# A feed-forward's second pair of column chunks in seven products, with block sums moved from VectorE to GpSimd

## Chip, core and metric

The kernel runs on one core of a Trainium2 chip. The time is device microseconds (us) from the first to the last instruction of one execution, with a small fixed part around it. Three runs of the kernel before took 1752.14, 1753.64 and 1753.94 us; the median is 1753.64 us.

## What is computed

Two layers, each with two feed-forwards around a mixer, all in float32, for 512 tokens of 1024 channels; a feed-forward is 2816 wide. This document is about the feed-forwards, four in the program:

```python
def swiglu_ffn(x, w_gu, w_down):
    a, u = jnp.split(x @ w_gu, 2, axis=-1)
    return (jax.nn.silu(a) * u) @ w_down
...
x = layer_norm(DEEPNORM_ALPHA * x + 0.5 * swiglu_ffn(x, ffn1_w_gu[l], ffn1_w_down[l]), ln1_g[l], ln1_b[l])
x = layer_norm(DEEPNORM_ALPHA * x + hybrid_mixer(x, w_in[l], w_out[l], ...), ln2_g[l], ln2_b[l])
x = layer_norm(DEEPNORM_ALPHA * x + 0.5 * swiglu_ffn(x, ffn2_w_gu[l], ffn2_w_down[l]), ln3_g[l], ln3_b[l])
```

## The kernel before

**Three matmuls for one.** Each operand is held as a high part (`uh` for weights, `xh` for x) and the rest of it (`ul`, `xl`). `split` (L171) makes them: ScalarE casts the high part (L173), VectorE subtracts it from the source (L174). A product is then three matmuls per 128x128 block of weights (`mm3`, L188 to L190): high by high, high by low, low by high.

**A feed-forward's first half.** It goes over 11 pairs of column chunks (`fp`). A pair is two chunks of 128 columns of the gate weights `a`, and two of the up weights `u`; the two arrive as two tiles `raw` of 1 MB, for which there are two buffers, and are split into `units` (six pairs of buffers). Loads are issued by SyncE as a buffer of `raw` comes free. An ordinary product of one chunk with all of x takes 8 x 3 matmuls, 512 tokens wide, or twice as many that are 256 wide.

**Seven products.** For the pairs in `SEVEN`, `glu7` takes a 2x2 block scheme (channels in halves, tokens in halves, columns in halves) with seven block products in place of eight, each of 4 x 3 matmuls 256 wide, once for `a` and once for `u`: 168 matmuls. It needs sums of the weights' blocks (tile `S`, four of 128x512 for each `raw`, L321 to L326), and sums of the blocks of x (`Th`, `Tl`; T1 to T4). The latter are made once in a feed-forward by `sums_of_x`: four tensors `xh + xl` (L556), four subtractions (L560), four splits. They lie in a part of `hT` that is written late.

**The start of a feed-forward**, where the change is. x arrives in four blocks of 128 tokens from the norm of the stage before, 0 to 3. For each, VectorE adds the residual (L513), takes statistics (L515, L518, L519), GpSimd makes the inverse root `rs` (L521), VectorE finishes `Y` (L522, L525), TensorE transposes it (L488), and `xh`, `xl` are split from the PSUM bank. So that TensorE need not wait for blocks 2 and 3, pair 0 (and half of pair 1) is taken on the first 256 tokens first: 96 narrow matmuls. Then come the transposes of blocks 2 and 3, or of 3 alone, then 192 narrow matmuls (the rest of pair 0, both halves of two chunks of pair 1), then the last two chunks of pair 1 in 48 matmuls that are 512 wide. From pair 2 on it is seven products. At its first matmul stand four throw-away ones (L460), which mark where pair 1 ends.

**Order of the work.** Every engine takes its instructions in a fixed order, which the tile framework made when the program was built, with a wait on other engines where one is needed: an instruction that waits holds up all behind it on its engine. GpSimd's list held, around a feed-forward, only the `rs` of the norms, and later the DMAs that add blocks of the down weights (L394). The 8 banks of PSUM are handed on: a transposed block needs a bank that an earlier gate (`silu(a) * u`, L630 and L631) has read. The first gate also waits until the norm before has let go of the memory that its parameters `ln` lie in, since the pools of the two stages share it.

Of the kernel before, what the change touches and what calls it, by code (L numbers as in the profile page):

```python
# [99 lines left out]
class Trunk:  # L100
# [199 lines left out]
    def seven_items(self, a, u):  # L300
# [16 lines left out]
        def s12(q):  # L317
            def go(v, hi, lo):
                s = sums[q] = self.spool.tile([P, 4, KC // 2, P], F32, tag="S", name=self.nm("S"), bufs=2)
                a11, a12, a21, a22 = blocks(v)  # L320
                self.nc.vector.tensor_add(s[:, 0], a21, a22)  # L321
# [214 lines left out]
    def ffn(self, g_, b, out=None):  # L536
        nc, tc, W = self.nc, self.tc, self.W
        with ExitStack() as ctx:
# [8 lines left out]

            def sums_of_x():

                x = hT[:, NF - KC :, :]  # L550
                B = [[x[:, i * H : (i + 1) * H, j * 256 : (j + 1) * 256] for j in range(2)] for i in range(2)]
                for i in range(2):
                    ks = slice(i * H, (i + 1) * H)
                    for j in range(2):
                        ts = slice(j * 256, (j + 1) * 256)
                        nc.vector.tensor_add(B[i][j], self.xh[:, ks, ts].bitcast(F32), self.xl[:, ks, ts].bitcast(F32))  # L556
                        yield 1
                for i, (dst, p_, q_) in enumerate(((B[0][0], B[0][1], B[0][0]), (B[0][1], B[1][1], B[0][1]),
                                                   (B[1][1], B[1][1], B[0][0]), (B[1][0], B[1][0], B[1][1]))):
                    nc.vector.tensor_sub(dst, p_, q_)  # L560
                    self.split(Th[:, i], Tl[:, i], dst)
                    yield 1
# [640 lines left out]
```

## Time and profile before

| | |
|---|---|
| median of the runs | 1753.64 us |
| the profiled execution | 1752.16 us, its span 1750.4 us |
| TensorE busy, granted clock | 1739.2 us, 0.999 |
| VectorE, ScalarE, GpSimd busy | 1415.5, 927.6, 182.7 us |

The profile is one execution as the hardware recorded it. A row of a timeline is: start and length in us, engine (PE is TensorE, DVE VectorE, ACT ScalarE, POOL GpSimd, SPq the queue of SyncE), line, operation, what it writes and reads, how many were merged, and in brackets for how long the engine had stood idle and who ended that. Operations of one engine that follow each other overlap a little in these records, so that two merged rows show better than one what each costs. A row of the windows gives each engine's busy time, with the number of instructions, in a stretch of the span. A row of the groups ends in busy us and mean ns of one.

The four feed-forwards are called F1 to F4 here. F1 follows the input, F2 and F4 a mixer, F3 the down projection of F2.

### The profile page before, as it was taken

To read this page: it belongs to the slowest core of one execution; us is meant where nothing else is said; L and a number is where in the kernel's file an instruction comes from. 1 tells how busy PE (TensorE), PEld (TensorE's weight loads), DVE (VectorE), ACT (ScalarE), POOL (GpSimd) and SP (SyncE) were. 2 spreads that over 40 slices of the span, in tenths; PEclk is the share of its full clock that TensorE was granted. 3 is DMA by queue.
4 is the path that set the end of the run, shared out by engine and by line. 5 is a ranking of instruction groups with operands and counts; after the bars stand their busy time and mean duration, and the time that the engine had idled before them with its cause. 6 is when DMAs were issued, how large, how long until landed. Compare 5 with 4: busy or idle time off the path is not lost.

```text
span 1750.4 us, 29200 instructions
## 1 busy us (share of the span) xinstructions
PE 1739.2 (99%) x11946; PEld 1580.1 (90%) x11946; DVE 1415.5 (81%) x1975; ACT 927.6 (53%) x1456; POOL 182.7 (10%) x154
## 2 busy tenths in 40 slices
PE   9999999999999999999999999999999999999998
PEld 9999988887789999998899999889877899999886
DVE  7888888856757889879898988988567587988887
ACT  5455656378712455555435556554785234555551
POOL 0000032111111000014000000312011110000231
PEclk9999999999999999999999999999999999999999
DMA  6234389323222243279423334982233123334891
GB/s 193 97 108 134 126 214 220 98 86 95 73 74 73 74 141 101 97 219 217 130 67 109 115 97 157 219 190 91 92 89 97 49 91 103 98 98 144 209 212 48
DMA packets 163765, 216.34 MB, mean 124 GB/s; under 512 B 5168, under 2 KB 116528, under 8 KB 163632
## 3 DMA queue, kind: packets, MB, share of 16 engines
q1 hardware_dynamic: 141872, 172.55, 30.5%
q0 software_dynamic: 21760, 41.95, 13.2%
q8 instruction: 93, 1.52, 0.4%
q14 instruction: 40, 0.33, 0.1%
HBM read 212.38 MB, written 2.10 MB: 123 GB/s over the span
## 4 chain that ended last, share of the span: by engine, by line
PE 48%; DVE 2%; DMA 0%; issue 0%; ACT 0%; POOLq 0%; DVEq 0%; ACTq 0%
PE ps L188 15%; PE ps L189 15%; PE ps L190 15%; PE ps L488 0%; DMA raw<-in_ffn_w_gu_dram 0%; PE ps L1030 0%; PE ps L995 0%; PE ps L1082 0%; PE ps L1022 0%; DVE Y L522 0%; PE ps L1044 0%; DVE ul L174 0%; DVE st L515 0%; DVE Y L513 0%; DVE xl L174 0%; DVE Y L525 0%
## 5 line engine op out<-in xcount | busy, mean ns | idle before, releaser
L188 PE MATMUL ps<-xh,uh 128*128 128x256 f32 (+1 forms) x1616 | 476.0, 295 | 0.0
L189 PE MATMUL ps<-xl,uh 128*128 128x256 f32 (+1 forms) x1616 | 473.0, 293 | 0.5 <-DVE xl L174 0.4
L190 PE MATMUL ps<-xh,ul 128*128 128x256 f32 (+1 forms) x1616 | 473.1, 293 | 0.4 <-DVE ul L174 0.4
L173 ACT CAST uh<-raw 128x1024 fp32r<-128x1024 f32 (+1 forms) x274 | 236.6, 884 | 233.3 <-PE ps L189 127.7
L174 DVE TENSOR_TENSOR ul<-raw,uh 128x1024 fp32r<-128x1024 f32 (+1 forms) x274 | 273.6, 1014 | 56.8 <-ACT uh L173 56.4
L188 PE MATMUL ps<-Th,uh 128*128 128x256 f32 x1152 | 318.0, 276 | 0.0
L189 PE MATMUL ps<-Tl,uh 128*128 128x256 f32 x1152 | 318.0, 276 | 0.0
L190 PE MATMUL ps<-Th,ul 128*128 128x256 f32 x1152 | 318.0, 276 | 0.0
L188 PEld LDWEIGHTS ps<-xh,uh 128*128 128x128 f32 x1616 | 304.1, 188 | 10.5 <-issue 1.6
L190 PEld LDWEIGHTS ps<-xh,ul 128*128 128x128 f32 x1616 | 303.5, 188 | 10.3 <-DVE ul L174 0.8
L189 PEld LDWEIGHTS ps<-xl,uh 128*128 128x128 f32 x1616 | 304.3, 188 | 9.1 <-DVE xl L174 0.9
L188 PE MATMUL ps<-uh,xh 128*128 128x512 f32 x720 | 285.2, 396 | 0.5 <-ACT xh L173 0.5
L189 PE MATMUL ps<-ul,xh 128*128 128x512 f32 x720 | 282.6, 392 | 0.0
L190 PE MATMUL ps<-uh,xl 128*128 128x512 f32 x720 | 281.0, 390 | 0.0
L173 ACT CAST uh<-S 128x1024 fp32r<-128x1024 f32 x144 | 151.3, 1051 | 144.0 <-PE ps L189 140.3
L189 PEld LDWEIGHTS ps<-Tl,uh 128*128 128x128 f32 x1152 | 216.3, 188 | 0.0
L188 PEld LDWEIGHTS ps<-Th,uh 128*128 128x128 f32 x1152 | 216.2, 188 | 0.0
L190 PEld LDWEIGHTS ps<-Th,ul 128*128 128x128 f32 x1152 | 216.2, 188 | 0.0
L174 DVE TENSOR_TENSOR ul<-S,uh 128x1024 fp32r<-128x1024 f32 x144 | 176.0, 1222 | 48.9 <-ACT uh L173 48.4
L394 POOL DMA_DIRECT2D R<-in_ffn_w_down_dram x80 | 97.1, 1217 | 999.8 <-DVE ul L174 912.3
L174 DVE TENSOR_TENSOR ul<-R,uh 128x1024 fp32r<-128x1024 f32 x120 | 145.5, 1223 | 31.5 <-ACT uh L173 31.2
L173 ACT CAST uh<-R 128x1024 fp32r<-128x1024 f32 x120 | 124.8, 1047 | 75.1 <-DMA R<-in_ffn_w_down_dram 36.4
(147 smaller groups left out, 2379.9 us busy)
## 6 DMA issues: line engine op xcount, KB each, us to landing
raw<-in_ffn_w_gu_dram SPq DMA_DIRECT2D x86, 1024.0 KB, 5.3
R<-in_ffn_w_down_dram POOLq DMA_DIRECT2D x80, 512.0 KB, 7.9
raw<-in_w_in_dram SPq DMA_DIRECT2D x18, 1024.0 KB, 5.2
R<-in_ffn_w_down_dram SPq DMA_DIRECT2D x16, 1024.0 KB, 6.2
raw<-in_ffn_w_down_dram SPq DMA_DIRECT2D x12, 1024.0 KB, 7.2
R<-in_ffn_w_down_dram SPq DMA_DIRECT2D x8, 512.0 KB, 4.2
raw<-in_w_in_dram SPq DMA_DIRECT2D x8, 512.0 KB, 5.9
raw<-in_w_out_dram SPq DMA_DIRECT2D x8, 512.0 KB, 6.1
```

Of the source, the lines that this page charges most:

```text
L173: a = self.nc.scalar.copy(hi, src)
L174: b = self.low = self.nc.vector.tensor_sub(lo, src, hi.bitcast(F32))
L188: keep(mm(out, ah, bh, start=start, stop=False, **kw))
L189: keep(mm(out, ah, bl, start=False, stop=False, **kw))
L190: keep(mm(out, al, bh, start=False, stop=stop, **kw))
L394: self.nc.gpsimd.dma_start(src, rows(i, j, g * 2, 2), accum_op=ALU.add))
```

## The change

- Pair 1 joins `SEVEN`. Its two products on the first half of the tokens, for `a` and for `u` (48 narrow matmuls), are taken before the transposes of blocks 2 and 3 (in F2 and F4: after all transposes, before the second half of pair 0). The other ten follow the second half of pair 0.
- Pair 1's eight weight sums (L321 to L326) go to GpSimd, in all four feed-forwards. Those of pairs 2 to 10 stay on VectorE.
- Three of the four `xh + xl` go to GpSimd (`whole`, L551): two once blocks 0 and 1 are there, the third with blocks 2 and 3. One stays on VectorE.
- `sums_of_x` makes T1 and T2 first, with a spare tile, then T3, then T4, and `glu7` takes C's product with T1 ahead of A's with T2. T1 hangs on GpSimd's third sum.
- The gate's scratch tile is 256 wide and has the buffers of `s21`, not `Q`.

```diff
-SEVEN = (2, 3, 4, 5, 6, 7, 8, 9, 10)
+SEVEN = (1, 2, 3, 4, 5, 6, 7, 8, 9, 10)
...
-    def seven_items(self, a, u):
+    def seven_items(self, a, u, eng):
...
-                self.nc.vector.tensor_add(s[:, 0], a21, a22)
-                self.nc.vector.tensor_sub(s[:, 1], s[:, 0], a11)
+                eng.tensor_add(s[:, 0], a21, a22)
+                eng.tensor_sub(s[:, 1], s[:, 0], a11)
...
-                self.nc.vector.tensor_sub(s[:, 2], a11, a21)
-                self.nc.vector.tensor_sub(s[:, 3], a12, s[:, 1])
+                eng.tensor_sub(s[:, 2], a11, a21)
+                eng.tensor_sub(s[:, 3], a12, s[:, 1])
...
-            if fp == 0:
-                items += [a[0], u[0], a[1], u[1]]
-            else:
-                items += self.seven_items(a, u) if fp in SEVEN else a + u
+            items += self.seven_items(a, u, self.nc.gpsimd if fp == 1 else self.nc.vector) if fp in SEVEN else [a[0], u[0], a[1], u[1]]
...
+            def whole(eng, i, j):
+                ks, ts = slice(i * H, (i + 1) * H), slice(j * 256, (j + 1) * 256)
+                eng.tensor_add(B[i][j], self.xh[:, ks, ts].bitcast(F32), self.xl[:, ks, ts].bitcast(F32))
+
             def sums_of_x():
...
+                whole(nc.gpsimd, 0, 1)
+                whole(nc.vector, 1, 1)
+                nc.vector.tensor_sub(B[0][0], B[0][1], B[0][0])
+                self.split(Th[:, 0], Tl[:, 0], B[0][0])
+                nc.vector.tensor_sub(spare, B[1][1], B[0][0])
+                self.split(Th[:, 2], Tl[:, 2], spare)
+                yield 1
+                nc.vector.tensor_sub(B[0][1], B[1][1], B[0][1])
+                self.split(Th[:, 1], Tl[:, 1], B[0][1])
+                yield 2
+                nc.vector.tensor_sub(B[1][0], B[1][0], spare)
+                self.split(Th[:, 3], Tl[:, 3], B[1][0])
+                yield 1
...
+                yield
                 us = W.get()
                 u22 = W.get()
                 for m in range(2):
                     C.append(self.ps())
                     u = W.get() if m else us
+                    product(C[m], u, 0, T1)
+                    nc.scalar.copy(Q[m][:, 2], C[m][:, :256])
                     product(A[m], u, 1, T2, False)
                     nc.scalar.copy(Q[m][:, 1], A[m][:, :256])
-                    product(C[m], u, 0, T1)
-                    nc.scalar.copy(Q[m][:, 2], C[m][:, :256])
...
+            us = [W.get() for _ in range(4)]
+            self.pin = False
+            au = [us[0:2], us[2:4]]
+            self.finish(self.pend[:2])
+            for i in range(2):
+                whole(nc.gpsimd, i, 0)
+            for c in range(2):
+                glu(au[c], c, 0, 256)
+            ahead = glu7(1)
+            next(ahead)
+            self.finish(self.pend[2:])
+            self.pend = []
+            xs = self.spawn(sums_of_x(), 0)
+            self.run(xs)
+            for c in range(2):
+                glu(au[c], c, 256, SEQ)
+                W.done(2)
+            self.finish([xs])
+            for _ in ahead:
+                pass
+            for fp in range(2, NFP):
```

How this moves instructions is seen at three places. GpSimd at the start of F3, before: the four `rs` of the norm behind F2 (blocks 0, 1, 2, 3) stand together, between the DMAs of F2 and F3.

```order
L394 DMA R_8337<-in_ffn_w_down_dram 128x2x512
L521 TENSOR_TENSOR rs_8845<-mv_8842,mhalf 128x1
L521 TENSOR_TENSOR rs_8868<-mv_8865,mhalf 128x1
L521 TENSOR_TENSOR rs_9011<-mv_9008,mhalf 128x1
L521 TENSOR_TENSOR rs_9034<-mv_9031,mhalf 128x1
L394 DMA R_11585<-in_ffn_w_down_dram 128x2x512 x2
```

The same place now, from the `rs` of block 1 on (`raw_9028` and `raw_9060` are pair 1's `a` and `u`, `hT_9166` holds the sums of x).

```order
L518 TENSOR_TENSOR rs_8986<-mv_8983,mhalf 128x1
L321 TENSOR_TENSOR S_9307<-raw_9028 128x512
L325 TENSOR_TENSOR S_9307<-raw_9028 128x512
L322 TENSOR_TENSOR S_9307<-S_9307,raw_9028 128x512
L326 TENSOR_TENSOR S_9307<-raw_9028,S_9307 128x512
L551 TENSOR_TENSOR hT_9166<-xh,xl 128x4x256 x2
L321 TENSOR_TENSOR S_9446<-raw_9060 128x512
L325 TENSOR_TENSOR S_9446<-raw_9060 128x512
L322 TENSOR_TENSOR S_9446<-S_9446,raw_9060 128x512
L326 TENSOR_TENSOR S_9446<-raw_9060,S_9446 128x512
L518 TENSOR_TENSOR rs_9127<-mv_9124,mhalf 128x1
L518 TENSOR_TENSOR rs_9150<-mv_9147,mhalf 128x1
```

All eight weight sums and two sums of x stand between the `rs` of block 1 and that of block 2.

VectorE in F2, before, from the last gate of pair 0's first half on: the sums of x and of the next weights, each made on VectorE itself.

```order
L631 SCALAR_TENSOR_TENSOR hT_5623<-ps_5694,Q_5757 128x256
L321 TENSOR_TENSOR S_5946<-raw_5610 128x512
L174 TENSOR_TENSOR xl<-ps_5743,xh 128x4x128
L174 TENSOR_TENSOR xl<-ps_5750,xh 128x4x128
L556 TENSOR_TENSOR hT_5623<-xh,xl 128x4x256 x2
L560 TENSOR_TENSOR hT_5623<-hT_5623 128x4x256
L322 TENSOR_TENSOR S_5946<-S_5946,raw_5610 128x512
L560 TENSOR_TENSOR hT_5623<-hT_5623 128x4x256
L174 TENSOR_TENSOR Tl_5625<-hT_5623,Th_5624 128x1024
```

The same place now, up to the split of T2 and T3; L557 waits for GpSimd's third sum of x.

```order
L551 TENSOR_TENSOR hT_5680<-xh,xl 128x4x256
L557 TENSOR_TENSOR hT_5680<-hT_5680 128x4x256
L600 TENSOR_TENSOR Q_5821<-Q_5821,ps_5820 128x256
L174 TENSOR_TENSOR ul_5848<-S_5849,uh_5847 128x1024
L174 TENSOR_TENSOR Tl_5682<-hT_5680,Th_5681 128x1024
L174 TENSOR_TENSOR ul_5888<-raw_5653,uh_5887 128x512
L174 TENSOR_TENSOR ul_5888<-raw_5659,uh_5887 128x512
L600 TENSOR_TENSOR Q_5861<-Q_5861,ps_5860 128x256
L559 TENSOR_TENSOR hT_5680<-hT_5680 128x4x256
L562 TENSOR_TENSOR hT_5680<-hT_5680 128x4x256
L174 TENSOR_TENSOR ul_5959<-S_5960,uh_5958 128x1024
L174 TENSOR_TENSOR Tl_5682<-hT_5680,Th_5681 128x1024 x2
```

Nine instructions now stand behind the wait for GpSimd and ahead of T2's split.

ScalarE in F1, before, from the first unit of pair 1 on: the four casts of blocks 2 and 3 come right behind two casts of weights.

```order
L173 CAST uh_176<-raw_168 128x1024
L173 CAST uh_180<-raw_168 128x1024
L173 CAST xh<-ps_292 128x4x128
L173 CAST xh<-ps_299 128x4x128
L173 CAST xh<-ps_306 128x4x128
L173 CAST xh<-ps_313 128x4x128
```

Now (`raw_168` and `raw_174` are pair 1's `a` and `u`, `S_322` the sums of `a` that GpSimd makes):

```order
L173 CAST uh_176<-raw_168 128x1024
L173 CAST uh_180<-raw_174 128x1024
L596 COPY Q_294<-ps_292 128x256
L173 CAST uh_320<-S_322 128x1024
L596 COPY Q_334<-ps_332 128x256
L173 CAST uh_360<-raw_168 128x512
L173 CAST uh_360<-raw_174 128x512
L173 CAST xh<-ps_367 128x4x128
L173 CAST xh<-ps_374 128x4x128
L173 CAST xh<-ps_381 128x4x128
L173 CAST xh<-ps_388 128x4x128
```

Two copies and three casts of weights, one of GpSimd's sums, are now ahead of the casts of x; F3 has the same order.

More of the change, by code (lines that the diff above doesn't have):

```diff
@@ L546, in ffn @@
             Tl = gp.tile([P, 4, H, 256], F32R, name=self.nm("Tl"))
-            def sums_of_x():
[L550 to L562, printed above, removed]
+            x = hT[:, NF - KC :, :]
+            B = [[x[:, i * H : (i + 1) * H, j * 256 : (j + 1) * 256] for j in range(2)] for i in range(2)]
+            spare = hT[:, NF - KC - H : NF - KC, :256]
+            def whole(eng, i, j):
+                ks, ts = slice(i * H, (i + 1) * H), slice(j * 256, (j + 1) * 256)
+                eng.tensor_add(B[i][j], self.xh[:, ks, ts].bitcast(F32), self.xl[:, ks, ts].bitcast(F32))
+            def sums_of_x():
+                whole(nc.gpsimd, 0, 1)
[11 more added lines that the diff above has]
+                yield 1
             def product(out, u, ui, b, new=True):
@@ L587, in glu7 @@
                     u = W.get()
-                    if fp == SEVEN[0] and m == 0:
+                    if fp == SEVEN[1] and m == 0:
                         self.lead(A[m], u)
@@ L628, in gate @@
             def gate(f, a, u, t0, t1):
[L629 to L632 removed]
+                sa = gp.tile([P, 256], F32, tag="s21", name=self.nm("s21"), bufs=2)
+                nc.scalar.activation(sa, a[:, :256], AF.Silu)
@@ L634, in glu @@
+                nc.vector.scalar_tensor_tensor(out=hT[:, f, t0:t1], in0=u[:, :256], scalar=0.5,
+                                               in1=sa, op0=ALU.mult, op1=ALU.mult)
             def glu(au, f, t0, t1):
                 a, u = self.ps(), self.ps()
-                self.projs(a[:, : t1 - t0], au[0], t0, t1)
-                self.projs(u[:, : t1 - t0], au[1], t0, t1)
+                self.projs(a[:, :256], au[0], t0, t1)
+                self.projs(u[:, :256], au[1], t0, t1)
                 gate(f, a, u, t0, t1)
-            for fp in range(NFP):
-                if fp == 0:
-                    us = [W.get() for _ in range(6)]
-                    self.pin = False
-                    au = [us[0:2], us[2:4]]
-                    self.finish(self.pend[:2])
-                    more = []
-                    for t0 in (0, 256):
-                        for c in range(2):
-                            glu(au[c], c, t0, t0 + 256)
-                            if t0:
-                                W.done(2)
-                        self.finish(self.pend[2:])
-                        if not t0:
-                            xs = self.spawn(sums_of_x(), 1)
-                        self.pend = []
-                        more.append(self.ps())
-                        self.projs(more[-1][:, :256], us[4], t0, t0 + 256)
-                    W.done()
-                    continue
-                if fp == 1:
-                    a1, u0 = us[5], W.get()
-                    for i in range(2):
-                        t0 = i * 256
-                        u = self.ps()
-                        self.projs(u[:, :256], u0, t0, t0 + 256)
-                        gate(2, more[i], u, t0, t0 + 256)
-                    W.done()
-                    u1 = W.get()
-                    glu((a1, u1), 3, 0, SEQ)
-                    W.done(2)
-                    continue
@@ L675, in ffn @@
                     self.split(*(v.rearrange("p g f t -> p (g f) t") for v in hv), hT[:, HALF : HALF + 4, :256])
-                if fp in SEVEN:
-                    self.finish([xs])
-                    glu7(fp)
-                    continue
-                a0, a1, u0 = W.get(), W.get(), W.get()
-                glu((a0, u0), fp * 2, 0, SEQ)
-                W.done(2)
-                u1 = W.get()
-                glu((a1, u1), fp * 2 + 1, 0, SEQ)
-                W.done(2)
+                for _ in glu7(fp):
+                    pass
             gctx.close()
```

4 lines of the change are left out of this document (removed).

## Prediction

> **What bounds the kernel now.** I read the page first: TensorE's share, and whether its dearest matmuls wait; then the windows of single stages, for what a matmul costs in each.
>
> ```profile
> span 1750.4 us, 29200 instructions
> PE 1739.2 (99%) x11946; PEld 1580.1 (90%) x11946; DVE 1415.5 (81%) x1975; ACT 927.6 (53%) x1456; POOL 182.7 (10%) x154
> L188 PE MATMUL ps<-Th,uh 128*128 128x256 f32 x1152 | 318.0, 276 | 0.0
> ...
> 100.00:150.00 50.00, 50.00 (x444) 50.00 (x443) 44.53 (x68) 28.37 (x43) 0.00 (x0) 1.00 0.29 93
> 584.51:595.71 11.20, 11.20 (x50) 9.03 (x49) 4.91 (x8) 2.69 (x4) 0.00 (x0) 1.00 0.57 187
> ```
>
> TensorE is busy 1739.2 of 1750.4 us, and its matmuls on `Th` have no idle time (0.0) ahead of them. So the kernel is bound by the number of matmuls, and whatever idles TensorE for a moment goes straight to the end: behind a feed-forward's start nothing has slack to give it back. In the steady stage of seven products (100 to 150) VectorE is busy 44.5 of 50 us, so it has little to spare either.
>
> A narrow matmul (256 tokens) costs 50 / 443 = 0.113 us. The window from 584.51 to 595.71 is F2's 48 wide ones (512 tokens): 11.20 / 48 = 0.233 us, somewhat more than two narrow ones.
>
> **What the change saves.** Pair 1 takes 96 narrow matmuls and 48 wide ones now: 96 x 0.113 + 11.20 = 22.05 us. In seven products it takes 168 narrow ones: 168 x 0.113 = 18.98 us. That is 3.07 us in each feed-forward, 12.3 us in four, if no wait is added.
>
> **What it puts on GpSimd.** Eight weight sums and three sums of x, per feed-forward. GpSimd makes none today; the nearest rows are its products in the mixer, of 512 and of 256 elements.
>
> ```profile
> L974 POOL TENSOR_TENSOR sw<-sw,retS 128x512 f32<-128x512 f32 x16 | 20.8, 1298 | 152.7 <-ACT sw L972 152.7
> L974 POOL TENSOR_TENSOR sw<-sw,ropeS 128x256 f32<-128x256 f32 x16 | 11.9, 745 | 46.4 <-ACT sw L972 46.4
> L321 DVE TENSOR_TENSOR S<-raw 128x512 f32<-128x512 f32 x72 | 49.6, 689 | 1.6 <-DMA raw<-in_ffn_w_gu_dram 0.3
> ...
> 842.32 2.35 DVE L174 TENSOR_TENSOR ul<-R,uh 128x1024 fp32r<-128x1024 f32 x2
> 8.40 1.28 DVE L174 TENSOR_TENSOR xl<-ps,xh 128x512 fp32r<-128x512 f32 x2
> ```
>
> A weight sum (512) costs GpSimd 1.30 us; a sum of x (1024) by the same slope 1.30 + 2 x (1.298 - 0.745) = 2.40 us, an estimate from these two rows. Eight and three are 17.6 us. On VectorE, back to back, a 512 costs 1.28 - 0.69 = 0.60 us and a 1024 costs 2.35 - 1.22 = 1.13 us, so VectorE is relieved of 8 x 0.60 + 3 x 1.13 = 8.2 us. That would be worth having where it is late, were the two engines free of each other. These rows say they are not:
>
> ```profile
> 374.96 0.69 DVE L973 TENSOR_TENSOR rr<-ps,ropeC 128x512 f32<-128x512 f32 x1 [1.68 <-ACT sw L972]
> 375.65 1.21 DVE L174 TENSOR_TENSOR ul<-raw,uh 128x512 fp32r<-128x512 f32 x1
> ...
> 375.00 1.31 POOL L974 TENSOR_TENSOR sw<-sw,ropeS 128x512 f32<-128x512 f32 x1 [4.77 <-ACT sw L972]
> ...
> 548.23 1.28 DVE L522 SCALAR_TENSOR_TENSOR Y<-Y,mv,ln 128x1024 f32<-128x1024 f32 x1
> 548.39 1.52 POOL L521 TENSOR_TENSOR rs<-mv,mhalf 128x1 f32<-128x1 f32 x1 [12.28 <-DVE mv L519]
> 557.12 1.27 DVE L522 SCALAR_TENSOR_TENSOR Y<-Y,mv,ln 128x1024 f32<-128x1024 f32 x1
> 557.35 1.46 POOL L521 TENSOR_TENSOR rs<-mv,mhalf 128x1 f32<-128x1 f32 x1 [7.43 <-DVE mv L519]
> ```
>
> The split at 375.65 reads two tensors from SBUF and takes 1.21 us where a 512 takes 0.69: it ends at 376.86, which is 0.55 us after GpSimd's product ended (376.31). It got nothing done beside GpSimd. L973, which reads PSUM and one tensor from SBUF, took its usual 0.69 under the same product. The other way round, `rs` ends 0.40 us after VectorE's L522 (549.51 to 549.91) and 0.42 after it (558.39 to 558.81), whichever head start L522 had. So an operation of VectorE with two inputs in SBUF and one of GpSimd run one after the other. I take that for all of the 11 new ones: weights' splits, sums, L522 and L525 are of that kind, splits and gates out of PSUM are not.
>
> [...]
>
> **F3, walked on the trace's clock.** The rows that it starts from and is compared with:
>
> ```profile
> 871.05 2.00 ACT L173 CAST uh<-raw 128x1024 fp32r<-128x1024 f32 x2 [5.18 <-DMA raw<-in_ffn_w_gu_dram]
> 879.54 1.45 POOL L521 TENSOR_TENSOR rs<-mv,mhalf 128x1 f32<-128x1 f32 x1 [16.16 <-DVE mv L519]
> 887.09 1.28 DVE L525 SCALAR_TENSOR_TENSOR Y<-Y,rs,ln 128x1024 f32<-128x1024 f32 x1
> 887.71 1.91 PE L488 MATMUL ps<-ident,Y 128*128 128x128 f32 x16
> 888.45 0.66 ACT L630 ACTIVATE Q<-ps 128x256 f32<-128x256 f32 x2 [14.44 <-PE ps L488]
> 872.95 1.06 ACT L173 CAST xh<-ps 128x512 fp32r<-128x512 f32 x2
> 922.93 0.64 PE L460 MATMUL ps<-uh 128*128 128x256 f32 x4
> ```
>
> GpSimd can start when pair 1's `a` lands, 871.0. Ahead of block 2's `rs` stand 8 x 1.30 + 2 x 2.40 = 15.2 us, and VectorE's two splits and L522 (L519 in the new file) get between: 2 x 1.13 + 1.2 = 3.5. So 889.7, and `rs` is out at 890.1 where it was out at 881.0. VectorE waits for it, and block 3's statistics' end is queued behind: 1.2 for block 2's finish, 0.2 for the mean, 1.2 for L522, 0.4 for `rs`, 1.2 for the finish: 894.3, where L525 ended at 888.4. The gates wait for this (`ln`'s memory), the transposes for the gates' banks. On ScalarE then, in its order: two gates 0.7, copy 0.3, a cast 0.95, copy 0.3, two casts of 512 0.5 each, two of x at 0.5: VectorE's third `xl`, which the second half's second matmul needs, ends near 900.1. TensorE, with 48 matmuls more ahead of it, is through at 887.7 + 48 x 0.113 = 893.1: it is late by 7.0 us, of which transposes fill 1.7 (887.71 to 889.4). Behind it stand 96 + 120 matmuls: 216 x 0.113 = 24.4, so 924.5 against 922.93 (L460). F3: **+1.6 us**. Without any blocking, 3.5 fall away and the path is 921.0: -1.9.
>
> **F2 and F4**, by F2's rows:
>
> ```profile
> 544.05 1.27 DVE L174 TENSOR_TENSOR xl<-ps,xh 128x512 fp32r<-128x512 f32 x2
> 558.91 1.28 DVE L525 SCALAR_TENSOR_TENSOR Y<-Y,rs,ln 128x1024 f32<-128x1024 f32 x1
> 561.02 1.03 PE L488 MATMUL ps<-ident,Y 128*128 128x128 f32 x8
> 595.71 0.64 PE L460 MATMUL ps<-uh 128*128 128x256 f32 x4
> ```
>
> Two sums of x go from 544.65 to 550.6 (2 x 2.40, a split of 1.13 between); L522, `rs` and block 2's finish follow, to 553.6. Block 3: 0.6 + 0.6 + 1.13 + 0.6 + 1.13 + 0.2, then 1.2 + 0.4, then a weight sum of 1.30 that gets in first, then 1.2: 562.0 (558.91 + 1.28 = 560.2 today). The transposes lose 1.0. GpSimd, from 559.5, has 8 x 1.30 + 2.40 = 12.8 with 3.5 of VectorE between: its last sum, for T1, is done at 575.8. L557 to 576.9; the nine behind it are 2 x 0.34 + 3 x 1.13 + 2 x 0.60 + 2 x 1.13 = 7.5; T2's split 1.13: 585.5. TensorE, from 562.0, has 0.8 of transposes and 48 + 96 + 12 matmuls (17.6) ahead of T2: 580.4. It waits 5.1, then 108 matmuls, 12.2: 597.7 against 595.71. F2: **+2.0**, and F4, in the same order, the same. Without blocking T2 is ready at 579.6, and F2 ends at 591.8: -3.9.
>
> **F1.**
>
> ```profile
> 12.58 1.23 DVE L174 TENSOR_TENSOR ul<-raw,uh 128x1024 fp32r<-128x1024 f32 x1 [0.95 <-ACT uh L173]
> 19.74 2.00 ACT L173 CAST uh<-raw 128x1024 fp32r<-128x1024 f32 x2 [1.89 <-DMA raw<-in_ffn_w_gu_dram]
> 20.10 1.91 PE L488 MATMUL ps<-ident,Y 128*128 128x128 f32 x16
> 55.61 0.64 PE L460 MATMUL ps<-uh 128*128 128x256 f32 x4
> ```
>
> Two sums of x (4.8) hold up the splits of pair 0, whose second (12.58 + 1.23 = 13.8) frees the buffer for pair 1: it ends between 13.9 and 16.2, and pair 1, here at 19.7, comes 0.1 to 2.3 later. Today the transposes cover that load at 20.10; now pair 1's products stand ahead of them and wait, to 22.3 (19.85, a weight sum of 1.30 and the split's 1.13). The first `a` ends at 25.0, `u`'s split, behind three weight sums, at 26.05; 48 matmuls are through at 28.5, the transposes at 30.2. On VectorE each of two splits of weights waits behind a sum (1.30 + 0.6, twice), then three `xl`: 34.1. 216 matmuls more: 58.5 against 55.61, **+2.9** (+4.0 if the load is at its late end; -0.4 without blocking).
>
> **Sum.** 2.9 + 2.0 + 1.6 + 2.0 = +8.5 on the profiled execution's 1752.16: 1760.7. That execution is 1.5 below the median of the runs, 1753.64, so 1762.1; I say **1762**. Priced at nothing: the scratch tile (same instructions), the spare tile and T1 before T2 (the same four subtractions and splits), L460 (it stays). Pairs 2 to 10 and the down projection are untouched.
>
> **Rivals.** (1) *The two engines hardly block each other*, or GpSimd's sums are quicker than its products: -0.4 - 3.9 - 1.9 - 3.9 = -10.1, or 1743.5; at most the full 12.3, 1741.3. It decides in F2 at T2: TensorE is there at 580.4, T2 at 579.6 without blocking; half of the 5.9 us of blocking would bring F2 back to about -1, and the total to no change. Against it are the four pairs of rows; for it, that no row shows a long list of GpSimd's beside a long one of VectorE's. (2) *Waits and savings cancel*: VectorE, relieved of 8.2 us, wins most of the turns: within 3.5 us of 1753.6. (3) *TensorE runs slow after its waits*, making things worse.
>
> ```profile
> 1.45 3.36 PE L480 MATMUL ps<-ident 128*128 128x128 f32 x14 [1.45 <-POOL ident masks.py:199]
> ```
>
> At the span's start 14 matmuls took 3.36 us, 0.24 each, where the 16 transposes from 887.71 took 1.66, 0.10 each. If the four idle stretches of 4 to 7 us bring that back for 3.4 us each, half of it is lost: 4 x 1.7 = 6.8, so 1769. The granted clock shows no such place today. [...]
>
> **How the numbers follow.** My forecast (1757 to 1767) 0.61; (1) 0.16; (2) 0.17; (3) 0.06. A measurement can tell 0.2%, 3.5 us. Slower by more: 0.61 + 0.06 = 0.67; the same 0.17; faster 0.16. The range leaves out the better end of (1) and the worse of (3): 1746 to 1769.
>
> **What would show it.** Right: VectorE's splits of 1024 at 2 to 3.5 us beside GpSimd's sums; in F3 `rs` of block 2 ten microseconds after its mean; TensorE waiting 3 to 6 us for `xl` in F1 and F3 and for `Tl` in F2 and F4; pair 1's end 1 to 4 us later each time. Wrong: splits of 1.22 beside GpSimd's sums, or pair 1's end earlier in F2.

## The result and the profile after

The changed kernel takes 1794.48 us (median of four executions, 1790.10 to 1797.24) against 1753.63 of the kernel before: a ratio of 1.0232, 95% interval 1.0208 to 1.0257. It is slower by 40.9 us, where 8.5 had been forecast. The profiled execution took 1792.28 us, its span 1790.5. (Of two kernels below, and of the kernel before beside them, one execution each was disturbed; these are left out of all ranges.)

The page of the kernel after: TensorE is still busy 98% of the span, 18 us more than before, though it has fewer columns to pass.

```profile
span 1790.5 us, 29516 instructions
PE 1757.4 (98%) x12042; PEld 1603.4 (90%) x12042; DVE 1442.2 (81%) x2003; ACT 947.2 (53%) x1492; POOL 264.6 (15%) x198
```

Where the time went is read from the marks at the end of pair 1 (before at 55.61, 595.71, 922.93 and 1463.06), and from windows over the four starts, from the first narrow matmul of the feed-forward to that mark. These are the marks and the windows of the kernel after.

```profile
64.86 0.63 PE L457 MATMUL ps<-uh 128*128 128x256 f32 x4
618.32 0.64 PE L457 MATMUL ps<-uh 128*128 128x256 f32 x4
949.76 0.64 PE L457 MATMUL ps<-uh 128*128 128x256 f32 x4
1496.52 0.63 PE L457 MATMUL ps<-uh 128*128 128x256 f32 x4
```

```profile
7.88:64.86 56.98, 49.12 (x378) 47.67 (x377) 47.19 (x53) 27.91 (x42) 21.56 (x11) 0.91 0.40 124
564.95:618.32 53.37, 47.79 (x377) 46.59 (x376) 44.28 (x56) 21.86 (x34) 18.89 (x12) 0.94 0.27 88
899.00:949.76 50.76, 47.31 (x377) 46.87 (x376) 41.28 (x55) 19.63 (x32) 15.38 (x10) 0.93 0.17 54
1443.19:1496.52 53.33, 47.40 (x377) 46.11 (x376) 44.26 (x56) 21.82 (x34) 18.89 (x12) 0.94 0.27 88
```

The third number is TensorE's busy time, the one before the last two the granted clock. Before, it stood at 1.00 until the last 4 us of the program, where TensorE had nothing left to do; now it falls below 1 in each start. F1's mark is 9.2 us later. F2 takes 53.37 us to its mark, where 595.71 - 549.03 = 46.68 were needed, F3 and F4 likewise: +6.7, +4.2, +6.6. The four starts make 26.8 us.

The rest is in stretches that the change does not touch. From the mark to the last product of pair 10 it was 171.86 us in every feed-forward before (from the start of the throw-away matmuls to the first wide one of the down projection). Now F2 and F3 take 171.86 still, F1 and F4 178.55. The windows show it as a count: how many narrow matmuls fit into 25 or 50 us.

```profile
75.00:100.00 25.00, 25.00 (x215) 25.00 (x214) 21.84 (x33) 13.17 (x22) 0.00 (x0) 1.00 0.26 85
650.00:700.00 50.00, 50.00 (x444) 50.00 (x443) 44.20 (x67) 27.60 (x42) 0.00 (x0) 1.00 0.40 127
970.00:1020.00 50.00, 50.00 (x444) 50.00 (x443) 44.48 (x65) 27.91 (x43) 0.00 (x0) 1.00 0.33 105
1530.00:1580.00 50.00, 50.00 (x427) 50.00 (x426) 42.48 (x65) 26.86 (x40) 0.00 (x0) 1.00 0.40 127
```

444 matmuls in 50 us are 0.113 us each; 427 are 0.117 (as are 215 in 25 us), at a granted clock of 1.00 and with TensorE busy throughout. In the starts of single matmuls there are just two steady spacings, 113.3 and 117.7 ns, and nothing between. Two stretches at 117.7 cost 2 x 6.7 = 13.4 us. 26.8 + 13.4 = 40.2, and the span grew by 40.1.

**F2, looked into.** GpSimd's list, VectorE's rows and TensorE's waits, from the last rows of block 3 on. The offset to the kernel before is 564.95 - 549.03 = 15.92.

```profile
576.89 1.29 POOL L321 TENSOR_TENSOR S<-raw 128x512 f32<-128x512 f32 x1 [1.52 <-DVE Y L522]
578.13 2.28 POOL L325 TENSOR_TENSOR S<-raw 128x512 f32<-128x512 f32 x1
...
588.86 2.40 POOL L551 TENSOR_TENSOR hT<-xh,xl 128x1024 f32<-128x1024 f32 x1
```

```profile
591.29 1.23 DVE L557 TENSOR_TENSOR hT<-hT 128x1024 f32<-128x1024 f32 x1 [8.53 <-POOL hT L551]
...
599.98 2.35 DVE L174 TENSOR_TENSOR Tl<-hT,Th 128x1024 fp32r<-128x1024 f32 x2
...
614.47 0.41 DVE L616 TENSOR_TENSOR Q<-Q,ps 128x256 f32<-128x256 f32 x1
...
617.87 0.41 DVE L620 TENSOR_TENSOR Q<-Q,ps 128x256 f32<-128x256 f32 x1
```

```profile
598.92 0.38 PE L188 MATMUL ps<-Th,uh 128*128 128x256 f32 x1 [2.21 <-ACT Th L173]
601.25 0.58 PE L189 MATMUL ps<-Tl,uh 128*128 128x256 f32 x1 [1.94 <-DVE Tl L174]
608.50 0.39 PE L188 MATMUL ps<-Th,uh 128*128 128x256 f32 x1 [0.41 <-ACT Q L610]
614.94 0.38 PE L188 MATMUL ps<-Th,uh 128*128 128x256 f32 x1 [0.71 <-DVE Q L616]
```

VectorE stood idle 8.53 us for GpSimd's last sum. From 591.29 on it has no idle time until 618.28, and its last addition for pair 1 (L620) ends 0.04 us before the mark. TensorE waits for T2 until 601.25, and again behind it, for VectorE's additions.

### The profile page after: what moved, and what is told of

Same layout as the page of the kernel before. It is cut to its first block, busy times and chain, and to the rows that moved or that the text cites. A ratio compares the mean times of both kernels' runs of the same rounds, so it can differ in the third digit from the quotient of the medians.

```text
span 1790.5 us, 29516 instructions
## 1 busy us (share of the span) xinstructions
PE 1757.4 (98%) x12042; PEld 1603.4 (90%) x12042; DVE 1442.2 (81%) x2003; ACT 947.2 (53%) x1492; POOL 264.6 (15%) x198
## 4 chain that ended last, share of the span: by engine, by line
PE 45%; DVE 3%; POOL 2%; issue 0%; DMA 0%; ACT 0%; POOLq 0%; DVEq 0%; ACTq 0%
PE ps L188 14%; PE ps L189 14%; PE ps L190 14%; DVE ul L174 1%; POOL hT L551 0%; DVE Y L522 0%; POOL S L325 0%; DVE Y L519 0%; PE ps L1017 0%; PE ps L982 0%; PE ps L1069 0%; POOL S L326 0%; PE ps L1009 0%; POOL S L321 0%; PE ps L485 0%
## 5 line engine op out<-in xcount | busy, mean ns | idle before, releaser
L188 PE MATMUL ps<-xh,uh 128*128 128x256 f32 (+1 forms) x1520 | 447.3, 294 | 4.5 <-ACT xh L173 2.8
L189 PE MATMUL ps<-xl,uh 128*128 128x256 f32 (+1 forms) x1520 | 444.3, 292 | 3.5 <-DVE xl L174 3.5
L190 PE MATMUL ps<-xh,ul 128*128 128x256 f32 (+1 forms) x1520 | 444.3, 292 | 3.4 <-DVE ul L174 3.4
L188 PE MATMUL ps<-Th,uh 128*128 128x256 f32 x1280 | 359.4, 281 | 7.6 <-ACT Th L173 4.4
L189 PE MATMUL ps<-Tl,uh 128*128 128x256 f32 x1280 | 359.2, 281 | 3.9 <-DVE Tl L174 3.7
L190 PE MATMUL ps<-Th,ul 128*128 128x256 f32 x1280 | 358.5, 280 | 0.0
L188 PEld LDWEIGHTS ps<-Th,uh 128*128 128x128 f32 x1280 | 242.6, 190 | 9.2 <-ACT Th L173 4.8
L189 PEld LDWEIGHTS ps<-Tl,uh 128*128 128x128 f32 x1280 | 242.5, 189 | 4.8 <-DVE Tl L174 4.8
L190 PEld LDWEIGHTS ps<-Th,ul 128*128 128x128 f32 x1280 | 245.0, 191 | 0.0
L174 DVE TENSOR_TENSOR ul<-S,uh 128x1024 fp32r<-128x1024 f32 x160 | 195.6, 1224 | 41.3 <-ACT uh L173 41.2
```

The lines of the kernel that those rows point to most:

```text
L174: b = self.low = self.nc.vector.tensor_sub(lo, src, hi.bitcast(F32))
L188: keep(mm(out, ah, bh, start=start, stop=False, **kw))
L189: keep(mm(out, ah, bl, start=False, stop=False, **kw))
L190: keep(mm(out, al, bh, start=False, stop=stop, **kw))
```

## The experiments

All of these go by the same account: the marks, the 171.86 or 178.55 us behind each, and the rest of the span, which did not change. For each kernel it is the profiled execution; the sums close on the span within 0.35 us. (e5 has no marks, and those of e12 stand elsewhere; they are not in the table.) Starts are longer (+) or shorter (-) than before, in us.

| kernel | F1 | F2 | F3 | F4 | stretches over 171.86 | span, less 1750.4 |
|---|---|---|---|---|---|---|
| after | 9.2 | 6.7 | 4.2 | 6.6 | F1, F4: 13.4 | 40.1 |
| e1, all sums on VectorE | 2.5 | 0.7 | -0.1 | 1.0 | F1, F2, F3, 1.2 in F4: 21.3 | 25.3 |
| e2, weight sums on VectorE | 5.1 | 2.6 | 0.7 | 2.7 | F1, F4: 13.4 | 24.4 |
| e3, sums of x on VectorE | 6.2 | 3.1 | 1.5 | 3.2 | F1, F3, F4: 20.1 | 34.3 |
| e4, wide throw-away matmuls | 9.9 | 7.6 | 4.8 | 7.6 | none | 29.8 |
| e6, e4 with a fill in F2, F4 | 9.9 | 8.8 | 4.4 | 8.8 | none | 31.8 |
| e7, e1 with one wide | 3.7 | 1.5 | 1.8 | 2.3 | 7.7 in F2, 0.1 in F4 | 17.0 |
| e8, e7 cutting less far ahead | 3.3 | -2.2 | 0.0 | -2.2 | 0.5 in F2, 6.5 in F4 | 5.9 |
| e9, e8 in F2 and F4 only | 0.6 | -1.5 | 0.3 | -0.7 | F4: 6.2 | 5.0 |
| e10, before with idle sums | 1.1 | 4.7 | 0.0 | 3.0 | none | 8.8 |
| e11, e4 with a fill in F1, F3 | 9.9 | 7.6 | 4.0 | 7.6 | none | 29.0 |

**Whose sums: e1, e2, e3.** The theory was that GpSimd's list, run by turns with VectorE, holds the starts up; the rival, that the new order does it whoever makes the sums.

e1 makes all three edits, e2 the first, e3 the second and the third.

```diff
-            items += self.seven_items(a, u, self.nc.gpsimd if fp == 1 else self.nc.vector) if fp in SEVEN else [a[0], u[0], a[1], u[1]]
+            items += self.seven_items(a, u, self.nc.vector) if fp in SEVEN else [a[0], u[0], a[1], u[1]]
...
-                whole(nc.gpsimd, 0, 1)
+                whole(nc.vector, 0, 1)
...
-                whole(nc.gpsimd, i, 0)
+                whole(nc.vector, i, 0)
```

> The changed kernel with all eleven sums of each feed-forward (eight weight sums, three sums of x) back on VectorE: seven products in pair 1, T1 before T2 and the rest of the order stay. The changed kernel's trace shows 25.4 us of idle TensorE in the four starts (1.0 before), 12.1 us lost in half-clock stretches behind it, and 13.4 us from narrow matmuls that go at 117.7 ns instead of 113.3 in pairs 2 to 10 of F1 and F4. Theory A, GpSimd's list is what idles TensorE: F2's last sum of x no longer comes at 591.3, VectorE's idle 8.5 us there takes the 5.9 us of sums, F2 and F4 lose no more than 1 us in waits, F1 and F3 together 6 or less, no half-clock stretch in F2, F3 and F4; 1747 to 1761 with 0 to 2 feed-forwards at 117.7 ns. Rival B, the new order (pair 1's products ahead of the transposes, VectorE's longer list) idles it whoever makes the sums: the waits and half-clock stretches stay, 1780 or more.

> The changed kernel with the eight weight sums back on VectorE; GpSimd keeps the three sums of x. Theory A: GpSimd's list shrinks from 17.6 us to 7.2, F2's last sum of x is done some 10 us earlier (near 565 on the clock of the kernel before) and T2 is not waited for; what stays is F1's first half, where two sums of x beside two splits idle TensorE 2.9 us, and a late rs in F3; idle time in the starts 5 to 10 us instead of 25.4, 1745 to 1765 with 0 to 2 feed-forwards at 117.7 ns. Rival B: 1780 or more.

> The changed kernel with the three sums of x back on VectorE; GpSimd keeps the eight weight sums. Theory A: F1's first half no longer waits (2.9 us back); in F2 and F4 the last weight sum ends 2.4 us or more earlier than the last sum of x did (591.3), and T2 comes earlier by about as much, so F2 and F4 still wait, 2 to 4 us each, and may still fall to half clock; idle time 10 to 16 us instead of 25.4, 1755 to 1780. Rival B: 1785 or more.

Measured: e1 1779.11 us, ratio 1.0146 (1.0131 to 1.0161); e2 1780.23, 1.0149 (1.0111 to 1.0186); e3 1786.71, 1.0182 (1.0157 to 1.0206). All three miss the theory's ranges. In e1 and e3 three stretches went at 117.7 ns, one more than allowed for; and in all three the 12.3 us saved on TensorE do not show. By their times e2 and e3 even lie where the rival had them, at 1780 or more and at 1785 or more, and e1 is 0.9 us short of it. The starts, not the times, tell the theories apart: 26.8 us with both lists on GpSimd, 14.0 without the sums of x, 11.0 without the weight sums, 4.1 with neither. So GpSimd's sums cost 22.7 of the 26.8, and the order by itself does not keep the waits. Why the saving is missing is seen in the window over e1's F2 and in TensorE's two waits there, 2.7 us where 1 or less was expected.

```profile
558.20:605.56 47.36, 44.67 (x378) 44.10 (x376) 47.06 (x63) 21.77 (x33) 2.33 (x2) 1.00 0.30 97
```

```profile
600.47 0.38 PE L188 MATMUL ps<-Th,uh 128*128 128x256 f32 x1 [0.76 <-DVE Q L616]
604.08 0.39 PE L188 MATMUL ps<-Th,uh 128*128 128x256 f32 x1 [1.93 <-DVE Q L616]
```

VectorE is busy 47.06 of 47.36 us, and TensorE waits out what it saves. (e8 below asks whether the length of VectorE's list is at fault or its order.)

**The blocking alone: e10.** The kernel before, with five sums on GpSimd that nobody waits for.

```diff
+                        if t0 == 0 and self.extra:
+                            for _ in range(5):
+                                nc.gpsimd.tensor_add(spare, self.xh[:, :H, :256].bitcast(F32), self.xl[:, :H, 256:].bitcast(F32))
```

> The kernel before, and in F2 and F4 alone five more sums of 1024 on GpSimd from the moment x is there, 12.0 us by 2.40 each, into memory that nobody reads; nothing waits for them and the orders of the other engines stay. It asks about the blocking alone. Theory, an operation of GpSimd and one of VectorE with two inputs in SBUF run one after the other: the sums take 3.4 to 3.6 us beside VectorE's of 1024, VectorE's 2.3 to 3.6 where it took 1.2; VectorE loses about 10 us, of which its idle time at the end of pair 1, 3.0 and 3.6 us, takes 6.6: F2 and F4 some 3 to 5 us longer each, 1760 to 1764. Rival, no blocking, only GpSimd's list being late in the changed kernel: VectorE's operations keep their 1.2 us and F2 and F4 their length, 1753.4.

Measured: 1763.28 us, ratio 1.0060 (1.0045 to 1.0076); F2 4.7 and F4 3.0 longer, F3 unchanged (F1, not edited, shows by its 1.1 how much the input's arrival varies). In F2 3.4 us at half the granted clock follow the wait, in F4 none do; that may be the difference between the two. VectorE and GpSimd in F2 of this kernel:

```profile
565.20 6.39 DVE L557 TENSOR_TENSOR hT<-xh,xl 128x1024 f32<-128x1024 f32 x2
571.52 3.41 DVE L561 TENSOR_TENSOR hT<-hT 128x1024 f32<-128x1024 f32 x1
574.85 2.89 DVE L322 TENSOR_TENSOR S<-S,raw 128x512 f32<-128x512 f32 x1
577.67 3.41 DVE L561 TENSOR_TENSOR hT<-hT 128x1024 f32<-128x1024 f32 x1
581.00 1.21 DVE L174 TENSOR_TENSOR Tl<-hT,Th 128x1024 fp32r<-128x1024 f32 x1
```

```profile
564.77 15.22 POOL L656 TENSOR_TENSOR hT<-xh,xl 128x1024 f32<-128x1024 f32 x5 [5.06 <-DVE xl L174]
```

Five sums of VectorE's fill the time of five of GpSimd's, one by one: 3.41 where it takes 1.21 alone, and 15.2 us where GpSimd's five would be 12.0 at 2.40 each. As soon as GpSimd is done, VectorE is back at 1.21. The blocking is shown for these sums: GpSimd's and VectorE's, each with both inputs in SBUF, took turns, as the prediction had read it from four pairs of rows. The rival is out.

**The two spacings: e4, e5.** In e4 four wide throw-away matmuls stand ahead of the four narrow ones at pair 1's end; in e5 the kernel before loses its four.

```diff
+        for _ in range(4):
+            self.tc.keep_in_program_order(
+                self.nc.tensor.matmul(out, u[0][:, 0, :], u[0].rearrange("p k c -> p (k c)")[:, :512],
+                                      start=True, stop=True, skip_group_check=True))
```

```diff
-                    if fp == SEVEN[0] and m == 0:
+                    if False:
```

> The changed kernel with four more throw-away matmuls, wide ones, ahead of the four at the end of pair 1 (+0.9 us in each feed-forward, 3.6 in all). Before the change, pair 1 ended in wide matmuls and pairs 2 to 10 went at 113.3 ns in all four feed-forwards; since, it ends in narrow ones, and F1 and F4 go at 117.7 ns. Theory: the spacing is drawn anew where TensorE's stream is broken, and what stands ahead of the break decides; with wide matmuls there again all four go at 113.3: 1794.5 - 13.4 + 3.6 = 1784.7. Rival: the spacing has to do with what runs beside it, or with chance from run to run: F1 and F4 stay at 117.7 ns, or others take it, 1791 to 1798.

> The kernel before without its four throw-away matmuls at the end of pair 1 (16 in all, 1.8 us). It asks about the spacing alone, with nothing of the change in it. Theory, the spacing is drawn where TensorE's stream is broken, and wide matmuls ahead of the break give 113.3 ns: pair 1 still ends in wide ones, so all four stretches stay at 113.3: 1751.8. Rival, the throw-away matmuls are what sets 113.3: without them one to four of the stretches (1510 narrow matmuls each) go at 117.7 ns, 6.7 us each: 1758.5 to 1778.6.

Measured: e4 1781.37 us (1780.20 to 1781.99), ratio 1.0158 (1.0143 to 1.0173); its span is 10.3 us shorter than that of the kernel after, where 13.4 - 3.6 = 9.8 were expected. The same two stretches as above, in e4:

```profile
75.00:100.00 25.00, 25.00 (x223) 25.00 (x222) 22.53 (x34) 14.14 (x24) 0.00 (x0) 1.00 0.27 85
...
1530.00:1580.00 50.00, 50.00 (x444) 50.00 (x443) 44.66 (x67) 27.59 (x42) 0.00 (x0) 1.00 0.38 121
```

All four stretches are at 113.3 ns, with everything else as it was, and the 13.4 us are gone. e5 went between the two expectations: 1751.67 us (1750.37 to 1759.98), ratio 0.9998 (0.9987 to 1.0009). Eight of ten executions took 1750.4 to 1752.8 us, two took 1757.0 and 1760.0, and the profiled one of these had F1 at 117.7. So the spacing can differ from one execution of the same kernel to the next, and wide matmuls ahead do not make 113.3 certain. The kernel before, with the wide ones and the throw-away four together, has it in all its executions here, to judge by their times (1751.3 to 1755.5).

**The half clock: e6, e11.** e4 with 20 narrow throw-away matmuls where TensorE waits: ahead of the wait for T1 in F2 and F4 (e6), behind the transposes in F1 and F3 (e11).

The first edit is e6's, the second e11's; `fill` is set in F2 and F4, and `throw` takes narrow matmuls of x with x into a bank that nobody reads.

```diff
+                    if fp == 1 and m == 0 and self.fill:
+                        self.throw(20)
                     product(C[m], u, 0, T1)
...
+            if not self.fill:
+                self.throw(20)
             for c in range(2):
                 glu(au[c], c, 256, SEQ)
```

> The kernel with the wide throw-away matmuls (1781.4), and 20 narrow ones more (2.3 us) in F2 and F4 where TensorE waits for T1, 2.5 us, just ahead of its 2.3 us wait for Tl. It asks about the half clock alone. Theory, the granted clock falls where too much of a short stretch is idle: with the first of the two waits filled F2 and F4 keep the full clock and lose no 2.8 and 1.6 us there; the waits for VectorE end where they did, 1777. Rival, the half clock has another cause: it stays, 1781 to 1783.

> The kernel with the wide throw-away matmuls (1781.4), and 20 narrow ones more (2.3 us) in F1 and F3, where TensorE waits 2.0 to 3.1 us for xh and xl behind the transposes. In F2 and F4 the same fill brought no time: half of the half-clock stretch went, and the time was lost again waiting for VectorE's additions, 1.2 us in each. Theory, in F1 and F3 VectorE is not what is late behind the fill, so the half clock's loss there (1.5 and 2.6 us) is on the path: F1 and F3 together 2 to 4 us shorter, 1777.4 to 1779.4. Rival, VectorE's backlog covers it there as well: 1781 to 1784.

Measured: e6 1783.64 us, ratio 1.0172 (1.0157 to 1.0187); e11 1781.19, 1.0160 (1.0146 to 1.0174). Neither theory held. The clock did rise (in F2 of e6 the half clock lasts 3.4 us, in e4 6.8; in F3 of e11 it is gone), and the time did not fall, but for 0.9 us in F3. In e6's F2 TensorE waits further on, for the copies and additions that stand in VectorE's and ScalarE's lists:

```profile
602.48 0.38 PE L188 MATMUL ps<-Th,uh 128*128 128x256 f32 x1 [1.34 <-ACT Q L623]
...
610.12 0.39 PE L188 MATMUL ps<-Th,uh 128*128 128x256 f32 x1 [1.09 <-DVE Q L629]
```

The two edits do not price the half clock alone, though: with the fill the fixed order of VectorE's and ScalarE's lists came out otherwise too. In F1 and F3 of e11 the additions of pair 1 stand elsewhere among pair 2's weight sums than in e4, and TensorE waits 1.55 us for one of them in each.

F1 is the same code in e4 and in e6. Its window in e4, then in e6, from 8.00 to the mark at 65.51 in both:

```profile
8.00:65.51 57.51, 48.15 (x385) 46.05 (x384) 48.69 (x53) 28.47 (x43) 21.57 (x11) 0.97 0.40 125
```

```profile
8.00:65.51 57.51, 49.59 (x379) 48.01 (x379) 47.66 (x53) 28.43 (x43) 21.40 (x11) 0.91 0.40 127
```

The clock was 0.97 once and 0.91 once, and pair 1 ended at the same hundredth. That alone does not show the half clock to be free, since `xl` was there 0.86 us earlier in e6 (37.39 against 38.25). Behind it e6 took 28.1 us with 5.8 at half clock and no wait, e4 27.3 with 3.0 at half clock and a wait of 0.15 for VectorE.

**Can the saving be had? e7, e8, e9, e12.** e7 is e1 with one wide throw-away matmul (the edit of e4 with `range(1)`). In e8 VectorE's additions come ahead of pair 2's weight sums. e9 takes e8's pair 1 in F2 and F4 only, with four wide ones, and the code before in F1 and F3. In e12 the eight throw-away matmuls of F2 and F4 stand at the end of pair 2.

The core of e8, of e9 (for F1 and F3) and of e12:

```diff
+            W.look = 3
             for _ in ahead:
                 pass
+            W.look = LOOK
...
+            if fp == 1 and key[1] == 0:
+                items += a + u
+                continue
...
-                    if fp == SEVEN[1] and m == 0:
+                    if fp == SEVEN[2 if self.whole else 1] and m == 0:
```

> All sums on VectorE, as in the first of these runs (1779.1, of which 19.2 us were F1, F2 and F3 at 117.7 ns), with one wide throw-away matmul ahead of the four at pair 1's end (0.9 us in all). Theory, what is left of the loss without GpSimd's sums is the spacing, drawn at the break: all four stretches at 113.3 ns, 1779.1 - 19.2 + 0.9 = 1760.8. Rival, one wide matmul does not set it, or the spacing belongs to the sums' place: 1767 to 1780.

> The same, and in the second half of pair 1 weights are cut three units ahead instead of six, so that VectorE's additions for pair 1's gates stand ahead of pair 2's weight sums. With all sums on VectorE, TensorE waited 0.9 and 2.1 us in F2, as much in F4 and 0.9 us in F3 for these additions, and VectorE had no idle time from 556 to 606. Theory, only the order of a full VectorE is at fault there: these 7 us go, 1754. Rival, VectorE is full whatever the order, and the waits move to pair 2's weights: 1760 to 1762.

> Seven products in pair 1 only where the look-ahead kernel gained by them: F2 and F4 as there, all sums on VectorE, with four wide throw-away matmuls instead of one; F1 and F3 word for word as in the kernel before. There F2 and F4 were 2.2 us shorter each, F1 and F3 3.3 and 0.6 us longer. Theory: 1753.4 - 2 x 2.2 + 2 x 0.7 (three more wide matmuls in F2 and F4) = 1750.4, faster by 0.17%, with all four stretches at 113.3 ns. Rival: a stretch is drawn at 117.7 in F2 or F4 all the same, +6 us in a share of the executions, and the median is 1753 or more.

> The mixed kernel (seven products in pair 1 of F2 and F4 alone, sums on VectorE), with the eight throw-away matmuls of F2 and F4 at the end of pair 2 instead of pair 1. There a wait of 0.1 us in pair 2 of F4, for an addition of VectorE's, was enough: 113.3 ns before it, 117.7 for the 1300 matmuls behind it, 5.8 us, and most executions ended near 1757, few near 1752. Theory, any break of the stream draws the spacing anew and the last one before a long unbroken stretch decides: set behind that wait, it is 113.3 to the end of pair 10 in most executions, and the median falls to 1751 to 1752.5, faster by 0.05 to 0.15%, with a quarter of the executions or fewer at 1757. Rival, the wait is not what draws it: the median stays near 1757.

Measured: e7 1769.09 us (1760.23 to 1771.38), ratio 1.0081 (1.0055 to 1.0106); e8 1755.04 (1751.55 to 1759.37), 1.0009 (0.9998 to 1.0020); e9 1757.16 (1751.76 to 1764.48), 1.0021 (1.0008 to 1.0033); e12 1753.47 (1752.16 to 1755.71), 1.0002 (0.9993 to 1.0010).

e7 missed: F2 went at 117.7, and three half-clock stretches came, where e1 had one, at F4's mark; F3 and F4 are 1.6 and 1.1 us longer than in e1, beside the 0.23 of the wide one, which may be theirs. F2 says little of the wide matmul: it and the four behind it ran at half clock there, and the 117.7 begins with the matmul at which the full clock returns (603.07). In e1's F4 the same return was followed by 113.3. e8 came out near its theory (1754) and shows the saving: the waits for additions in pair 1 are gone, so the order of VectorE's list was at fault more than its length. This is F2's window there, 44.41 us against 46.68, TensorE busy throughout. (Its profiled execution lost 7.0 us elsewhere, nearly all in F4's stretch.)

```profile
552.30:596.71 44.41, 44.41 (x378) 44.19 (x377) 44.08 (x60) 20.93 (x32) 2.32 (x2) 1.00 0.29 96
```

e9 went the rival's way: it lost the gain again in F4's pair 2. Here TensorE came a tenth of a us late, right behind the end of an addition of VectorE's (L624, to 1480.03), and these are the rows at that place, and the windows on both sides of it:

```profile
1479.88 0.28 PE L191 MATMUL ps<-Th,ul 128*128 128x256 f32 x1
1480.09 0.38 PE L189 MATMUL ps<-Th,uh 128*128 128x256 f32 x1
1480.31 0.28 PE L190 MATMUL ps<-Tl,uh 128*128 128x256 f32 x1
1480.43 0.28 PE L191 MATMUL ps<-Th,ul 128*128 128x256 f32 x1
```

```profile
1465.00:1479.00 14.00, 14.00 (x126) 14.00 (x125) 13.76 (x20) 8.39 (x13) 0.00 (x0) 1.00 0.45 151
1481.00:1495.00 14.00, 14.00 (x121) 14.00 (x120) 14.00 (x22) 8.25 (x13) 0.00 (x0) 1.00 0.39 131
```

Two matmuls come 0.21 and 0.22 us after the one before, and from then on some 1350 go at 0.118 instead of 0.113. Three of e9's eleven executions ended at 1751.8 to 1752.3, seven at 1756.6 to 1758.1, one at 1764.5: judged by these times, one stretch slow in most, two in one. e12 bears out half of its theory: with the throw-away matmuls behind that wait no execution is above 1755.71, and its profiled one has 113.3 from them on in all four. The forecast 1751 to 1752.5 was missed: its time is that of the kernel before. In its profiled execution pair 2 of F2 went at 117.7 ahead of the throw-away matmuls, and F4 waited 0.67 us for an addition. No kernel here is faster than the kernel before by more than the runs scatter.

## Why the prediction was wrong

**What held.** The prices: GpSimd's sums take 1.29 and 2.40 us (1.30 and 2.40 had been put down), and one of 512 takes 2.28 beside an operation of VectorE's. The blocking: e10. The saving of 3.07 us, nearly: e8's F2 is 2.2 shorter, with 0.23 spent on a wide matmul and 0.3 more than before on narrow ones at 117.7. F2's walk as far as T2: last sum of GpSimd's at 575.8 forecast, 591.26 - 15.92 = 575.3 measured; T2 ready at 585.5, measured 601.25 - 15.92 = 585.3. Part of this is luck: GpSimd began its weight sums 1.5 us later than forecast (576.89 - 15.92 = 561.0 against 559.5) and then lost 1.6 us to VectorE in place of 3.5. F3's walk as far as x (offset 899.00 - 876.40 = 22.60), by these rows of GpSimd, VectorE and TensorE:

```profile
910.01 0.55 POOL L518 TENSOR_TENSOR rs<-mv,mhalf 128x1 f32<-128x1 f32 x1
```

```profile
910.60 1.29 DVE L522 SCALAR_TENSOR_TENSOR Y<-Y,rs,ln 128x1024 f32<-128x1024 f32 x1 [7.32 <-POOL rs L518]
...
913.83 1.28 DVE L522 SCALAR_TENSOR_TENSOR Y<-Y,rs,ln 128x1024 f32<-128x1024 f32 x1 [0.45 <-POOL rs L518]
```

```profile
919.89 0.38 PE L188 MATMUL ps<-xh,uh 128*128 128x256 f32 x1 [2.02 <-ACT xh L173]
921.71 0.58 PE L189 MATMUL ps<-xl,uh 128*128 128x256 f32 x1 [1.44 <-DVE xl L174]
```

`rs` of block 2 is out at 888.0 (890.1 forecast), block 3 finished at 892.5 (894.3), the second half's second matmul starts at 899.1 (900.1). The waits came where they were forecast, though in two pieces each: 2.0 and 1.4 us in F3, 2.2 and 1.9 in F2.

**The step that failed** is the one behind these points, the same in all four sums: "It waits 5.1, then 108 matmuls, 12.2" in F2, "Behind it stand 96 + 120 matmuls" in F3, "216 matmuls more" in F1. I took TensorE as free to run, at 0.113 us a matmul, once T2 or `xl` was there. In F2 those 108 matmuls took 618.32 - 601.25 = 17.1 us, not 12.2; in F3 the 216 took 949.76 - 921.71 = 28.1, in F1 64.86 - 37.62 = 27.2, not 24.4.

In F2 and F4 VectorE ended the pair. It had been held up and had all its splits, subtractions and pair 2's weight sums still to do, ahead of the additions that TensorE needs: 27 us without a pause from 591.29 on. I followed VectorE's list to the operand that was waited for first, and not to the end of the pair. That is 4.7 of the 26.8 - 8.5 = 18.3 us in F2, and as much in F4.

In F1 and F3 TensorE did not wait again behind `xl`. There its rows show the half clock, from 37.62 to 43.53 and from 921.71 to 927.58, with a matmul every 0.213 us:

```profile
921.00:928.00 7.00, 6.29 (x31) 6.29 (x32) 6.93 (x7) 1.14 (x2) 2.37 (x1) 0.53 0.86 287
```

5.9 us at that rate cost 2.8 in each of the two. The other 188 matmuls of F3 went at 117.7 ns, 0.8 more. That covers F1's 27.2 and all but 0.1 of F3's 28.1; with F3's `xl` 1.0 us early, 2.6 of the 18.3 are left there. VectorE stood close behind: its last addition that TensorE needs ends at 62.79 and 947.47, 12 matmuls (1.4 us) follow, and ahead of it VectorE had paused for 0.3 and 0.8 us in all since `xl`. By these rows I estimate that with the full clock pair 1 would have ended at most 1 us earlier in F1, and 1.7 in F3.

**F1** failed earlier too, at its load. The split that frees pair 1's buffer ended at 15.96, as late as the forecast allowed (13.9 to 16.2); but the sum went by the early end, with the load at 19.85. It was issued at 15.99 instead of 13.84 and took 7.1 us to its first cast, where it had taken 5.9:

```profile
23.05 1.04 ACT L173 CAST uh<-raw 128x1024 fp32r<-128x1024 f32 x1 [2.84 <-DMA raw<-in_ffn_w_gu_dram]
```

```profile
24.15 0.39 PE L188 MATMUL ps<-xh,uh 128*128 128x256 f32 x1 [1.64 <-ACT uh L173]
...
37.62 0.58 PE L189 MATMUL ps<-xl,uh 128*128 128x256 f32 x1 [2.04 <-DVE xl L174]
```

`xl` is there at 37.6 instead of 34.1, and 3.2 of these 3.5 us are the load. (TensorE also waits 1.15 us twice in the first half, for pair 0's own low parts; that is not added, since behind it TensorE waits for this load all the same.) Behind `xl` come 27.2 us instead of 24.4. 3.5 + 2.8 are the 6.3 by which F1 (9.2) passed its 2.9.

**The rivals.** (1) and (2) are out. (3), the clock, happened in all four starts, once for 3.4 us and four times for 6.8, where I had put down four times 3.4. It had a chance of 0.06 and a price of 6.8 us in all. The prediction saw no such place in the trace before; there is one, at its end: TensorE's last matmul ends at 1742.2, and the clock is 0.50 from 1746.7 on. What the half clock cost is known only within bounds: nothing in F2 and F4, where TensorE waits for VectorE's additions behind it; at most 1 us in F1 and 1.7 in F3, by the estimate above; and at most 1.6 in a start of e7. TensorE's busy time makes it look like more, 191.6 us in the four windows above (49.12 + 47.79 + 47.31 + 47.40) for fewer columns than before.

**What no rival had** is the spacing: 13.4 of the 40.2 us, from matmuls that the change leaves alone. With the 18.3 us in the starts it makes up the whole miss. The prediction said that pairs 2 to 10 are untouched and priced the throw-away matmuls at nothing ("it stays"). They stay, but what stands ahead of them had been wide and is narrow now. The trace before held both spacings already. The prediction took 0.113 us from the window 100 to 150; in F2's start, where it used that price, 194 narrow matmuls took 22.70 us, 0.117 each:

```profile
561.81:584.51 22.70, 22.70 (x196) 22.70 (x194) 22.70 (x27) 10.92 (x15) 0.00 (x0) 1.00 0.15 48
```

What stays open: why the stream has two spacings, and what in a break picks one. The runs show where it can change and for how long it then stays, not by what.

## What to carry to other kernels

Follow the late engine's list to the end of the stage, not to the first operand that is waited for: work that is held up comes back as further waits. And price a matmul from the stage where it will run. An engine that takes turns with the busy one is no spare engine: some 33 us of VectorE's sums (4 x 8.2), put on GpSimd, made the starts 22.7 us longer. And where a stream of matmuls bounds a kernel, count how many fit into a window before and after, also in the stages that were not touched.
